# Weight tiles as contiguous blocks laid out by the host, sixteen k tiles by row halves at a part's begin, later square sums, in a three-part transformer block

## The chip, the cores and the metric

The kernel runs on one core of a Trainium2 chip. The metric is the device time of one execution in microseconds (us); before the change the median of three executions is 2004.15 us. All arithmetic is float32: every operand of a large matmul is split into a high and a low part, and one product is three matmuls (high·high, low·high, high·low).

## The reference, cut to what matters

One layer on 256 tokens of width 2048: a gated feed-forward part (FFN1), a mixer (an RWKV7 recurrence beside a pooling branch), and a second feed-forward part (FFN2), each between two RMS norms and with a residual.

```python
D_MODEL, SEQ, D_FF, RWKV_WIDTH, POOL_WIDTH = 2048, 256, 5632, 1024, 1024

def _rmsnorm(x, g):
    y = x * lax.rsqrt(jnp.mean(x * x, axis=-1, keepdims=True) + NORM_EPS)
    return y * g

def _swiglu(x, w_gate, w_up, w_down):
    return (jax.nn.silu(x @ w_gate) * (x @ w_up)) @ w_down

def _hybrid_mixer(u, w_in, ...):
    p = u @ w_in
    z_a, z_b, g_a, g_b = jnp.split(p, IN_SPLITS, axis=-1)
    y_a = _rwkv7_branch(z_a, ...) @ w_proj_a
    y_b = _pool_branch(z_b, pool_w, pool_scale) @ w_proj_b
    m = jax.nn.sigmoid(g_a) * y_a + jax.nn.sigmoid(g_b) * y_b
    return m @ w_out

h = h + 0.5 * _rmsnorm(_swiglu(_rmsnorm(h, ln_ffn1_pre), ffn1_gate, ffn1_up, ffn1_down), ln_ffn1_post)
h = h + _rmsnorm(_hybrid_mixer(_rmsnorm(h, ln_mix_pre), ...), ln_mix_post)
h = h + 0.5 * _rmsnorm(_swiglu(_rmsnorm(h, ln_ffn2_pre), ffn2_gate, ffn2_up, ffn2_down), ln_ffn2_post)
```

## The kernel before

**Tiling.** A weight matrix is used in tiles of 128 rows (one k tile) by 512 columns. Two k tiles make a pair of 512 KB. SyncE (SP) loads a pair into one of five `w32` buffers with one DMA, straight from the weight matrix, so that a partition receives two runs of 2 KB. ScalarE (ACT) casts it to the high part `wH`, VectorE (DVE) subtracts to get the low part `wL`, and TensorE (PE) multiplies it with the activations, two halves (h = 0, 1) of 128 tokens, which are the stationary operand. `wH` and `wL` have five buffers each; other tiles lie in 34 general "units" of 4 KB a partition.

**Feed-forward.** The gate and up matrices are worked in eleven column blocks b = 0 to 10 of 512 columns; gate is called `f`, up is called `l`. For some pairs of k tiles a block uses seven products in place of eight (a Strassen-like step over 2 k tiles x 2 column blocks; one such step is called a quad here). A quad saves one product, three matmuls, and costs DVE extra sums and differences of weights: `t13`, a difference into `va[:, 1]`, and `t4`. `GATE1` and `GATE2` give the number of quads of each block; the first half of a quad of block b (`early`) is worked in block b - 1, the other half (`late`) in block b. The down projection and the mixer's output projection use quads too (`quad`).

**A quad's loads.** `raw4` fills two `w32` buffers, `va` and `vb`, with four DMAs of 256 KB, one for each quarter tile; `late` loads two quarter tiles again.

**A part's begin.** The first gemm of the mixer and of FFN2 (`gemm_tok` with `lead`) works the first `LEAD` k tiles by halves of the tokens: all of them for h = 0, then all for h = 1 (`by_half`); pairs from `STAG` k tiles on are held in units and not in the `wH`/`wL` buffers.

**The head.** FFN1's first gemm starts cold (`head`): x comes transposed (`x_t`), one k tile of x with each weight tile, is scaled by the norm's gain and split. After k tile `SQ` = 11 the square sums of x for the norm are released: four squares on ACT, additions on DVE (`xq`), two small matmuls (`px`), and a power on GpSimd (POOL) that gives `rs`, with which gate's result leaves PSUM.

**What sets the order.** All operations are recorded, and `Plan.simulate` replays them with a cost model (rates of DMA and engines, deadlines, buffers) and so fixes, before the program is built, the order on each engine. On the chip each engine then works its list strictly in order, and waits on semaphores. In the profile nearly all operations therefore carry the one line L494 (the replay in `emit`); they are told apart by the names of their tiles.

Of the kernel before, what the change touches and what calls it, by code (L numbers as in the profile page):

```python
# [38 lines left out]
STAG = 8  # L39
LEAD = 12  # L40
# [9 lines left out]
GATE1 = [0, 0, 2, 4, 3, 4, 3, 4, 3, 4, 4]  # L50
GATE2 = [0, 0, 3, 4, 3, 4, 3, 4, 3, 4, 4]
# [4 lines left out]
SPARE = 1  # L56
HOLD = 3e5
# [9 lines left out]
ONES = 8  # L67
FIRST = 0.4

# [21 lines left out]
SYNC = 55.0  # L91
LAND = 1600.0
LANES = 8
CARRY = 1800.0
# [9 lines left out]
class Plan:  # L104
# [109 lines left out]
    def cost(s, o, name, w, r, k):  # L214
# [4 lines left out]
        if name == "dma_start":  # L219
            x = w[0]  # L220
            o.nbytes = math.prod(x.shape) * 4
            run = min(min(y.shape[-1] for y in w + r) * 4, 2048)
            o.dur = o.nbytes / (387.0 if run >= 2048 else 387.0 * max(run, 64) * 1.25
                                / (run + 512))
            o.pace = {"SP": 500.0, "ACT": 110.0, "POOL": 600.0}[o.eng]
            return
# [66 lines left out]
    def simulate(s):  # L293
# [23 lines left out]
        def can(o):  # L317
            for i in o.new:
# [189 lines left out]
class Block:  # L508
# [183 lines left out]
    def head(s, w, c0, KT, do, keep, xs):  # L692
# [20 lines left out]
        while k < KT:  # L713
            if k:
                first(load, k, n(k))
# [5 lines left out]
        for k in range(KT):  # L721
# [6 lines left out]
            if k == SQ:  # L728
                s.late = last
                with s.set(behind=last, lag=4000.0):  # L730
# [92 lines left out]
class Columns:  # L823
# [32 lines left out]
    def early(s, k):  # L856
        q = s.b
        V = q.nc.vector
        va, vb = q.raw4(k, s.wf, s.cf, s.wl, s.cl)
        t13 = q.unit((P, 2, 512), F32, "t13")  # L860
        V.tensor_tensor(out=t13, in0=va, in1=vb[:, :1].to_broadcast([P, 2, 512]),
# [3 lines left out]
        V.tensor_tensor(out=t4, in0=vb[:, 1], in1=va[:, 1], op=ALU.subtract)  # L865
# [9 lines left out]
    def late(s, k):  # L875
        q = s.b
        vc = q.raw().rearrange("p (a c) -> p a c", a=2)
        for i, (w, c0) in enumerate(((s.wf, s.cf), (s.wl, s.cl))):
# [1119 lines left out]
```

## Time and profile before

| | |
|---|---|
| Median of three executions | 2004.15 us (2002.16 to 2005.69) |
| The profiled execution: its own time, its span | 2001.42 us, 1999.6 us |
| PE busy | 1988.3 us (99%) |
| DVE busy | 1782.8 us (89%) |
| ACT busy | 1179.8 us (59%) |
| POOL busy | 75.4 us (4%) |
| Mean DMA rate | 239 GB/s |
| Granted TensorE clock | 0.999 |

A window row gives, for a stretch of the span, the busy time of each engine with its number of instructions, the granted clock, the share of time in which the 16 DMA engines were busy, and the rate. A matmul's shown duration (0.39 us) overlaps the next one, so a lost time on PE is read from the distance between starts; the timeline shows starts and durations, and in brackets the idle time ahead of an instruction with what ended it. A group row ends in busy time, mean ns of one, idle time before. A DMA row gives instructions, KB and median us from issue to landing.

### The profile page before, as it was taken

Reading aid. Unit: us, or ns where it says so; the run is one execution under the profiler, and the core shown is the slowest. Engines: PE = TensorE matmul, PEld = TensorE weight load, DVE = VectorE, ACT = ScalarE, POOL = GpSimd, SP = SyncE. Lnnn points to the kernel's source line nnn. Section 1 sums busy time; section 2 is a strip of 40 time slices with the busy share of each in tenths; the row PEclk is TensorE's granted clock in tenths of the full one; section 3 lists DMA queues with packets and bytes.
Section 4 is the critical chain, followed back from the end, with each engine's and each line's share of the span. In section 5 each row is a group of like instructions: output and inputs, shape, how many; then the busy total and the mean of one; then the engine's idle time right before and its main releaser. Section 6 shows DMA issues by size and latency. Waiting matters only on the chain.

```text
span 1999.6 us, 28096 instructions
## 1 busy us (share of the span) xinstructions
PE 1988.3 (99%) x9751; PEld 1641.3 (82%) x9751; DVE 1782.8 (89%) x2320; ACT 1179.8 (59%) x1557; POOL 75.4 (4%) x142
## 2 busy tenths in 40 slices
PE   9999999999999999999999999999999999999998
PEld 7888888888888888888888788888888888788886
DVE  8989999999989867898859879898999999998896
ACT  7555556566555656864646445575555655655563
POOL 0000000000000020002200100010000000000000
PEclk9999999999999999999999999999999999999999
DMA  8788888887667787767576567777888888976674
GB/s 282 237 261 267 279 264 283 267 283 229 219 197 255 235 261 233 216 194 244 151 218 183 177 202 228 259 233 244 266 278 262 272 282 274 281 225 212 200 253 147
DMA packets 263198, 477.47 MB, mean 239 GB/s; under 512 B 22928, under 2 KB 50832, under 8 KB 263056
## 3 DMA queue, kind: packets, MB, share of 16 engines
q1 hardware_dynamic: 259536, 466.11, 73.9%
q0 software_dynamic: 3232, 9.44, 1.4%
q8 instruction: 76, 1.25, 0.2%
q14 instruction: 66, 0.54, 0.1%
q10 hardware_dynamic: 288, 0.14, 0.0%
HBM read 447.94 MB, written 26.61 MB: 237 GB/s over the span
## 4 chain that ended last, share of the span: by engine, by line
PE 66%; DVE 15%; DMA 9%; issue 7%; ACT 2%; SPq 1%; POOL 0%; DVEq 0%; ACTq 0%; POOLq 0%
PE mm L494 25%; PE l L494 17%; PE f L494 15%; DVE wL L494 7%; DMA w<-in_ffn_gate_dram 6%; PE p L494 5%; DVE t L494 3%; DMA w<-in_ffn_up_dram 2%; ACT wH L494 2%; DVE w L494 1%; SPq L494 1%; DMA x<-cx 1%; DVE sg L494 1%; DVE hL L494 1%; DVE f L494 1%
## 5 line engine op out<-in xcount | busy, mean ns | idle before, releaser
L494 ACT CAST wH<-w 128x1024 fp32r<-128x1024 f32 (+2 forms) x720 | 745.3, 1043 | 627.7 <-PE mm L494 155.6
L494 DVE TENSOR_TENSOR wL<-w,wH 128x1024 fp32r<-128x1024 f32 (+2 forms) x720 | 860.0, 1206 | 135.0 <-ACT wH L494 130.7
L494 PE MATMUL l<-wL,xH 128*128 128x512 f32 x770 | 300.0, 390 | 0.0
L494 PE MATMUL l<-wH,xL 128*128 128x512 f32 x770 | 299.6, 389 | 0.0
L494 PE MATMUL l<-wH,xH 128*128 128x512 f32 x770 | 299.6, 389 | 0.0
L494 PE MATMUL mm<-wL,xH 128*128 128x512 f32 (+1 forms) x656 | 254.6, 388 | 1.1 <-DVE wL L494 1.0
L494 PE MATMUL mm<-wH,xH 128*128 128x512 f32 (+1 forms) x656 | 254.3, 388 | 0.3 <-ACT xH L494 0.3
L494 PE MATMUL mm<-wH,xL 128*128 128x512 f32 (+1 forms) x656 | 253.8, 387 | 0.0
L494 PE MATMUL f<-wL,xH 128*128 128x512 f32 x644 | 251.0, 390 | 0.4 <-DVE wL L494 0.3
L494 PE MATMUL f<-wH,xH 128*128 128x512 f32 x644 | 250.7, 389 | 0.0
L494 PE MATMUL f<-wH,xL 128*128 128x512 f32 x644 | 250.5, 389 | 0.0
L494 DVE TENSOR_TENSOR t<-w,w 128x1024 f32<-128x1024 f32 (+1 forms) x166 | 168.9, 1017 | 18.4 <-DMA w<-in_ffn_gate_dram 14.1
L494 PEld LDWEIGHTS l<-wL,xH 128*128 128x128 f32 x770 | 144.5, 188 | 31.5 <-DVE wL L494 1.5
L494 PEld LDWEIGHTS l<-wH,xL 128*128 128x128 f32 x770 | 144.6, 188 | 29.8
L494 PEld LDWEIGHTS l<-wH,xH 128*128 128x128 f32 x770 | 144.6, 188 | 29.8
L494 PEld LDWEIGHTS mm<-wL,xH 128*128 128x128 f32 x656 | 123.2, 188 | 26.4 <-DVE wL L494 2.4
L494 PEld LDWEIGHTS mm<-wH,xH 128*128 128x128 f32 x656 | 123.2, 188 | 25.1 <-ACT xH L494 0.7
L494 PEld LDWEIGHTS mm<-wH,xL 128*128 128x128 f32 x656 | 123.2, 188 | 24.3 <-DVE xL L494 0.2
L494 PEld LDWEIGHTS f<-wL,xH 128*128 128x128 f32 x644 | 120.9, 188 | 26.6 <-DVE wL L494 1.7
L494 PEld LDWEIGHTS f<-wH,xL 128*128 128x128 f32 x644 | 120.9, 188 | 25.2
L494 PEld LDWEIGHTS f<-wH,xH 128*128 128x128 f32 x644 | 120.9, 188 | 24.9
L494 DVE TENSOR_TENSOR wL<-t,wH 128x1024 fp32r<-128x1024 f32 x103 | 125.2, 1216 | 3.9 <-ACT wH L494 3.6
(310 smaller groups left out, 2778.8 us busy)
## 6 DMA issues: line engine op xcount, KB each, us to landing
w<-in_w_in_dram SPq DMA_DIRECT2D x128, 512.0 KB, 4.5
w<-in_ffn_up_dram SPq DMA_DIRECT2D x113, 512.0 KB, 4.7
w<-in_ffn_gate_dram SPq DMA_DIRECT2D x109, 512.0 KB, 4.8
w<-in_ffn_down_dram SPq DMA_DIRECT2D x104, 512.0 KB, 4.5
w<-in_ffn_gate_dram SPq DMA_DIRECT2D x197, 256.0 KB, 4.2
w<-in_ffn_up_dram SPq DMA_DIRECT2D x189, 256.0 KB, 4.2
w<-in_ffn_down_dram SPq DMA_DIRECT2D x144, 256.0 KB, 3.9
cx<-T SPq DMA_DIRECT2D x32, 512.0 KB, 3.6
```

The lines of the kernel that those rows point to most:

```text
L494: ins = o.fn(*[real(x) for x in o.a], **{n: real(x) for n, x in o.k.items()})
```

## The change

The host lays out every weight anew: a pair of k tiles by 512 columns is one contiguous block of 128 rows of 4 KB, so that each partition gets one run. For a quad there are three blocks, `(l0, f1)`, `(l1, f0)` and `(f1, l1)`; `raw4` needs two DMAs of 512 KB, `late` one. Gate and up lie in one array, and x is laid out as [128, 16 x 256]; `XLOADS` loads its k tiles in groups of 1, 2, 4, 4 and 4. The quads of a block are now also read by the host. `LEAD` goes from 12 to 16, `STAG` from 8 to 6. The last block has three quads and not four in both feed-forward parts, and FFN2's block 2 four and not three. In the head, the part of the square sums from the small matmuls on (`finish`) is recorded after the first gemm's matmuls. The planner's numbers change: DMA rate, the surcharge on carried tiles (`CARRY`), and a rule that keeps the last four free units from operations of the recurrence that run ahead of their turn.

```diff
-STAG = 8
-LEAD = 12
+STAG = 6
+LEAD = 16
-GATE1 = [0, 0, 2, 4, 3, 4, 3, 4, 3, 4, 4]
-GATE2 = [0, 0, 3, 4, 3, 4, 3, 4, 3, 4, 4]
+GATE1 = [0, 0, 2, 4, 3, 4, 3, 4, 3, 4, 3]
+GATE2 = [0, 0, 4, 4, 3, 4, 3, 4, 3, 4, 3]
+SPARE2 = 4
+XLOADS = {1: 1, 2: 2, 4: 4, 8: 4, 12: 4}
+SQLAG = 4000.0
+class Pairs:
+    def __init__(s, ap, KT, where):
+        s.ap, s.KT, s.where = ap, KT, where
+    def tile(s, b, k, i):
+        r = (b * s.KT // 2 + k // 2) * 3 + i
+        return s.ap[r * P:r * P + P]
+    def get(s, j, n, c0, cw):
+        b, side = s.where(c0 // 512)
+        return s.tile(b, j, side)[:, j % 2 * 512:j % 2 * 512 + n * 512]
+    def quad(s, k, c0, i):
+        return s.tile(s.where(c0 // 512)[0], k, i)
...
+RATE = 410.0
-CARRY = 1800.0
+CARRY = 2000.0
...
-                if i.tag == "u" and o.stream != "chain" and len(slots["u"]) <= SPARE:
+                if i.tag == "u" and len(slots["u"]) <= max(SPARE, SPARE2):
                     q = streams.get("chain")
-                    if q and q[0].nom <= o.nom < q[0].nom + HOLD:
+                    few = len(slots["u"]) <= SPARE
+                    if q and o.stream != "chain" and few and q[0].nom <= o.nom < q[0].nom + HOLD:
+                        return False
+                    if q and o.stream == "chain" and len(slots["u"]) <= SPARE2 \
+                            and o.nom > q[0].nom:
                         return False
...
     def get_w(s, w, j, n, c0, cw, own=False):
         w32 = s.raw(own)
-        s.nc.sync.dma_start(out=w32[:, :n * cw].rearrange("p (k c) -> p k c", k=n),
-                            in_=w[j * P:(j + n) * P, c0:c0 + cw]
-                            .rearrange("(k p) c -> p k c", p=P))
+        s.nc.sync.dma_start(out=w32[:, :n * cw], in_=w.get(j, n, c0, cw))
...
-            if k:
-                first(load, k, n(k))
+            if k in XLOADS:
+                first(load, k, XLOADS[k])
             first(get, k, n(k))
...
-    def raw4(s, k, wf, cf, wl, cl):
-        va, vb = [s.raw().rearrange("p (a c) -> p a c", a=2) for _ in range(2)]
-        for dst, kk, w, c0 in ((va[:, 0], k, wl, cl), (vb[:, 0], k, wf, cf),
-                               (va[:, 1], k + 1, wf, cf), (vb[:, 1], k + 1, wl, cl)):
-            s.nc.sync.dma_start(out=dst, in_=w[kk * P:kk * P + P, c0:c0 + 512])
-        return va, vb
+    def raw4(s, k, w, c0):
+        v = [s.raw() for _ in range(2)]
+        for i in range(2):
+            s.nc.sync.dma_start(out=v[i], in_=w.quad(k, c0, i))
+        return [t.rearrange("p (a c) -> p a c", a=2) for t in v]
...
-        V.tensor_tensor(out=t13, in0=va, in1=vb[:, :1].to_broadcast([P, 2, 512]),
+        V.tensor_tensor(out=t13, in0=va, in1=vb[:, 1:].to_broadcast([P, 2, 512]),
                         op=ALU.subtract)
         V.tensor_tensor(out=va[:, 1], in0=va[:, 0], in1=t13[:, 1], op=ALU.add)
         t4 = s.t4[k] = q.tmp("t4")
-        V.tensor_tensor(out=t4, in0=vb[:, 1], in1=va[:, 1], op=ALU.subtract)
+        V.tensor_tensor(out=t4, in0=vb[:, 0], in1=va[:, 1], op=ALU.subtract)
...
-        for i, (w, c0) in enumerate(((s.wf, s.cf), (s.wl, s.cl))):
-            q.nc.sync.dma_start(out=vc[:, i], in_=w[k * P + P:k * P + 2 * P, c0:c0 + 512])
-        b22, b21 = q.halves(vc)
+        q.nc.sync.dma_start(out=vc, in_=s.wf.quad(k, s.cf, 2))
+        b22, b21 = q.halves(vc.rearrange("p (a c) -> p a c", a=2))
...
-            return lambda h, ps: (pss[i].append(ps), h and ev("fl"[i], pss[i]))
+            return lambda h, ps: pss[i].append(ps)
         s.gemm_tok(wg, 0, at, NKD, hold(0), lead=True, xs=xs)
+        if xs:
+            xs[3]()
+        ev("f", pss[0])
         s.gemm_tok(wu, 0, at, NKD, hold(1))
+        ev("l", pss[1])
...
-                in_=x_t[k * P:(k + n) * P].rearrange("(k p) t -> p k t", p=P))
+                out=xT[k // 4].rearrange("p k t -> p (k t)")[:, k % 4 * S:(k % 4 + n) * S],
+                in_=x_t[:, k * S:(k + n) * S])
...
+            sq.append(a)
+
+        def finish():
+            a = sq[0]
             ps = s.psum("px")
```

What this does to the order on the engines is shown at three places. The first is VectorE in the head, where the last gate weights (`wL_70`, `wL_72`), the first up weights (`wL_86`, `wL_89`, `wL_92`), the additions of squares (`xq`) and the first step of the normalised activations (`nx`) meet. Before:

```order
L494 TENSOR_TENSOR wL_72_361<-w32_48_265,wH_71_352 128x1024
L494 TENSOR_TENSOR nx_125_370<-xH_5_168,xL_6_176 128x1024
L494 TENSOR_TENSOR xq_73_363<-xq_73_363,xq_74_372 128x1024
L494 TENSOR_TENSOR nx_129_389<-xH_7_215,xL_8_227 128x1024
L494 TENSOR_TENSOR xq_75_378<-xq_75_378,xq_76_385 128x1024
L494 TENSOR_TENSOR wL_86_406<-w32_84_276,wH_85_393 128x1024
L494 TENSOR_TENSOR xq_73_363<-xq_73_363,xq_75_378 128x1024
L494 TENSOR_TENSOR wL_89_423<-w32_87_290,wH_88_401 128x1024
```

VectorE at the same place now:

```order
L552 TENSOR_TENSOR wL_72_350<-w32_48_237,wH_71_338 128x1024
L552 TENSOR_TENSOR wL_86_357<-w32_84_247,wH_85_348 128x1024
L552 TENSOR_TENSOR nx_125_368<-xH_5_169,xL_6_178 128x1024
L552 TENSOR_TENSOR wL_89_379<-w32_87_257,wH_88_359 128x1024
L552 TENSOR_TENSOR xq_73_366<-xq_73_366,xq_74_376 128x1024
L552 TENSOR_TENSOR nx_129_398<-xH_7_222,xL_8_227 128x1024
L552 TENSOR_TENSOR xq_75_384<-xq_75_384,xq_76_393 128x1024
L552 TENSOR_TENSOR wL_92_419<-w32_90_272,wH_91_401 128x1024
```

The first two pairs of up weights now stand ahead of the additions of squares, and the four large additions stand behind them in front of the third pair.

The second place is SyncE's list of DMAs at the first quad of FFN1 (`w32_161` and `w32_162` are its two buffers `va` and `vb`; `cx0` and `x32_109` carry the block's result through memory). Before:

```order
L494 DMA w32_158_605<-in_ffn1_gate_dram 128x2x512
L494 DMA w32_161_626<-in_ffn1_up_dram 128x512
L494 DMA w32_161_626<-in_ffn1_gate_dram 128x512
L494 DMA cx0_87<-T1_108_635 128x1024
L494 DMA w32_162_655<-in_ffn1_gate_dram 128x512
L494 DMA w32_162_655<-in_ffn1_up_dram 128x512
L494 DMA x32_109_690<-cx0_87 32x4x256 x4
```

SyncE at the same quad now:

```order
L552 DMA w32_158_591<-in_gate_up1_dram 128x1024
L552 DMA cx0_87<-T1_108_620 128x1024
L552 DMA w32_161_641<-in_gate_up1_dram 128x1024
L552 DMA w32_162_649<-in_gate_up1_dram 128x1024
L552 DMA x32_109_673<-cx0_87 32x4x256 x4
L552 DMA w32_175_728<-in_gate_up1_dram 128x1024
```

Four issues of quarter tiles have become two of whole buffers, and the store of the carried tile has moved ahead of both.

The third place is GpSimd in the mixer, where the first recurrence's four powers (`g`) and the loads of the second recurrence's small weights (`w` from `rwkv_w`, `rwkv_a`, `rwkv_g`) share a queue. Before:

```order
L494 DMA w_2005_8741<-in_rwkv_w_dram 64x512 x2
L494 DMA w_2005_8741<-in_rwkv_a_dram 64x512 x2
L494 DMA w_2096_8768<-in_rwkv_g_dram 128x512
L494 DMA w_2096_8768<-in_rwkv_g_dram 32x512 x3
L494 DMA msp<-sgb_8255 128x512
L494 DMA w_2096_8768<-in_rwkv_g_dram 32x512
L494 COPY Z_7526<-ev_7516 64x256
L494 COPY Z_7526<-od_7520 64x256
```

GpSimd where the same loads stand now:

```order
L552 TENSOR_TENSOR g_1821_8951<-g_1820_8938,mhalf 128x4
L552 TENSOR_TENSOR g_1831_9043<-g_1830_9026,mhalf 128x4
L552 DMA w_1998_9061<-in_rwkv_w_dram 64x512 x2
L552 DMA w_1998_9061<-in_rwkv_a_dram 64x512 x2
L552 DMA w_2089_9091<-in_rwkv_g_dram 128x512
L552 DMA w_2089_9091<-in_rwkv_g_dram 32x512 x4
L552 MEMSET ev_9128 64x8x32
L552 MEMSET od_9136 64x8x32
L552 MEMSET Z_9147 128x512
L552 TENSOR_TENSOR g_1839_9158<-g_1838_9149,mhalf 128x4
```

The nine loads stood ahead of the recurrence's copies and powers and now stand behind its third power, in front of its fourth.

More of the change, by code (lines that the diff above doesn't have):

```diff
@@ L729, in head @@
                 s.late = last
-                with s.set(behind=last, lag=4000.0):
+                with s.set(behind=last, lag=SQLAG):
                     square()
@@ L1050, in down @@
     def down(s, wd, at, KT, ev, hT, sm, plan):
-        for c, (nq, first, step) in ((0, plan[0]), (2, plan[1])):
-            J = Columns(s, wd, c * 512, wd, c * 512 + 512, at, KT, sm,
-                        [2 * i for i in range(nq)], s.bank, s.psum)
+        for c, (nq, first, step), ks in zip((0, 2), plan, down_quads(plan)):
+            J = Columns(s, wd, c * 512, wd, c * 512 + 512, at, KT, sm, ks, s.bank, s.psum)
             quads = list(J.quads)
@@ L1876, in load @@
             if k is None:
[L1877 removed]
+                nc.scalar.dma_start(out=xT[0][:, 0], in_=x_t[:, :S])
                 nc.scalar.dma_start(out=ct[:, :16], in_=cols[:, :16])
@@ L1966, in laid_out @@
         o += n * P
-    return (("x_t", _np.ascontiguousarray(_np.asarray(inputs["x"])[0].T)),
-            ("cols", _np.ascontiguousarray(cols.reshape(NCOL, P).T)))
+    return (("x_t", _np.ascontiguousarray(rows(_np.asarray(inputs["x"])[0].T, 0, S))),
+            ("cols", _np.ascontiguousarray(cols.reshape(NCOL, P).T)),
+            *((n, _np.ascontiguousarray(v, _np.float32)) for n, v in big))
 def kernel(**inputs):
```

116 lines of the change are left out of this document (86 added, 30 removed).

## Prediction

> **What bounds the kernel now.** I read the page's shares first, then the windows by stage, then PE's waits, then the timeline at the places where PE lost time, and last what fed those places. The page:
>
> ```profile
> span 1999.6 us, 28096 instructions
> PE 1988.3 (99%) x9751; PEld 1641.3 (82%) x9751; DVE 1782.8 (89%) x2320; ACT 1179.8 (59%) x1557; POOL 75.4 (4%) x142
> PE 66%; DVE 15%; DMA 9%; issue 7%; ACT 2%; SPq 1%; POOL 0%; DVEq 0%; ACTq 0%; POOLq 0%
> ```
>
> PE is the bound over the whole span and DVE is close behind. The windows say how close PE is to its own pace:
>
> ```profile
> core 0: us, PE busy (x) PEld busy (x) DVE busy (x) ACT busy (x) POOL busy (x), PEclk, DMA share, GB/s
> 10.00:20.00 10.00, 9.43 (x42) 7.50 (x41) 8.23 (x15) 8.24 (x16) 0.00 (x0) 1.00 1.01 355
> 20.00:70.00 50.00, 49.45 (x220) 40.18 (x219) 49.55 (x60) 32.12 (x37) 3.17 (x5) 1.00 0.72 231
> 200.00:300.00 100.00, 100.00 (x442) 82.61 (x442) 93.38 (x105) 58.83 (x72) 0.00 (x0) 1.00 0.84 271
> 400.00:500.00 100.00, 99.84 (x439) 81.92 (x438) 95.95 (x112) 61.38 (x72) 0.00 (x0) 1.00 0.82 256
> 1697.00:1712.00 15.00, 15.00 (x67) 12.40 (x67) 13.04 (x16) 8.87 (x11) 0.00 (x0) 1.00 0.94 284
> 1700.00:1800.00 100.00, 99.26 (x435) 81.09 (x434) 95.68 (x111) 62.40 (x74) 0.00 (x0) 1.00 0.82 252
> ```
>
> In the undisturbed 200 to 300 us PE starts 442 matmuls in 100 us, one each 0.226 us, at the full granted clock. A change of layout cannot make a matmul shorter, so what can be won is time in which PE did not start one. Where it waited in the large products:
>
> ```profile
> PE mm L494 <- DVE wL L494: 1.0, 2, 0.6
> PE f L494 <- DVE wL L494: 0.9, 3, 0.6
> ```
>
> These sums are too small, because the shown 0.39 us of a matmul covers part of a wait. The true loss is the distance of two starts less 0.226:
>
> ```profile
> 17.01 0.39 PE L494 MATMUL mm<-wH,xH 128*128 128x512 f32 x1
> 17.97 0.50 PE L494 MATMUL mm<-wL,xH 128*128 128x512 f32 x1 [0.57 <-DVE wL L494]
> 28.75 0.39 PE L494 MATMUL mm<-wH,xH 128*128 128x512 f32 x1
> 29.59 0.50 PE L494 MATMUL mm<-wL,xH 128*128 128x512 f32 x1 [0.44 <-DVE wL L494]
> 65.67 0.39 PE L494 MATMUL f<-wH,xH 128*128 128x512 f32 x1
> 66.17 0.50 PE L494 MATMUL f<-wL,xH 128*128 128x512 f32 x1
> 420.63 0.40 PE L494 MATMUL f<-wH,xH 128*128 128x512 f32 x1
> 421.18 0.50 PE L494 MATMUL f<-wL,xH 128*128 128x512 f32 x1 [0.15 <-DVE wL L494]
> 1712.05 0.40 PE L494 MATMUL f<-wH,sH 128*128 128x512 f32 x1
> 1713.02 0.50 PE L494 MATMUL f<-wL,sH 128*128 128x512 f32 x1 [0.56 <-DVE wL L494]
> 1716.45 0.40 PE L494 MATMUL f<-wH,xH 128*128 128x512 f32 x1
> 1717.02 0.50 PE L494 MATMUL f<-wL,xH 128*128 128x512 f32 x1 [0.17 <-DVE wL L494]
> ```
>
> The losses are 0.73, 0.61, 0.27, 0.32, 0.74 and 0.34 us, and the matmul behind each wait takes 0.50 in place of 0.39, 0.11 more: 3.0 + 0.7 = 3.7 us in all, always for a low weight part from DVE. That is nearly everything outside the first matmul's wait and the tail, so 0.2% (4 us, about what a measurement of this kernel can tell from no change) is near the most that the profile offers.
>
> **The change part by part.** The sum is made against the profiled execution: 2001.42 us, of which 1999.6 are its span. The median of the runs shown is 2.7 us above it; I come back to that.
>
> *Quads.* FFN1 has one fewer: eight products for seven, three matmuls more, 3 x 0.226 = +0.7 us on PE, on the path. FFN2 moves one from block 10 to block 2: no matmul more or less.
>
> *Blocks 9, where the stalls of 420 and 1712 to 1717 us lie.* DVE had just lost time there to DMA:
>
> ```profile
> 412.95 0.69 DVE L494 TENSOR_TENSOR t<-w,w 128x512 f32<-128x512 f32 x1 [0.87 <-DMA w<-in_ffn_up_dram]
> 1708.80 0.69 DVE L494 TENSOR_TENSOR t<-w,w 128x512 f32<-128x512 f32 x1 [1.42 <-DMA w<-in_ffn_up_dram]
> DVE t L494 <- DMA w<-in_ffn_gate_dram: 14.1, 16, 1.6
> L494 DVE TENSOR_TENSOR t<-w,w 128x1024 f32<-128x1024 f32 x103 | 125.4, 1218 | 14.4 <-DMA w<-in_ffn_gate_dram 14.1
> ```
>
> Each time a `t4` waited for its last quarter tile 4 to 8 us before PE waited for DVE, while the DMA engines were 94% busy (1697 to 1712 us). The change works on both: block 9 now prepares three quads of block 10 and not four, which takes an early half (one difference of 1.22 us, two of 0.69, two low parts of 1.22, by these rows and that of 28.31 us below: 5.0 us of DVE work) and its 1 MB out of the block, and the last quarter comes with its block. Bounds: nothing of these 1.40 + 0.33 = 1.7 us goes, or all; the waits (0.87, 1.42) are smaller than the DVE work that leaves, so I take 1.6.
>
> *One block per load.* At full load the rate can be read:
>
> ```profile
> 22.00:27.00 5.00, 5.00 (x24) 4.14 (x23) 5.00 (x6) 5.00 (x6) 0.00 (x0) 1.00 1.03 394
> 1252.00:1254.00 2.00, 2.00 (x11) 1.65 (x10) 1.69 (x2) 0.84 (x3) 0.00 (x0) 1.00 1.02 416
> w<-in_ffn_gate_dram SPq DMA_DIRECT2D x109, 512.0 KB, 4.8
> w<-in_ffn_down_dram SPq DMA_DIRECT2D x104, 512.0 KB, 4.5
> w<-in_ffn_gate_dram SPq DMA_DIRECT2D x197, 256.0 KB, 4.2
> ```
>
> At 22 to 27 us all loads are pairs in runs of 2 KB (394 GB/s); at 1252 to 1254 us runs of 4 KB lie among them (416). So the new layout is worth 5% of DMA time or somewhat more, and PE does not wait for DMA itself. In undisturbed blocks it gives 0: what hides it is PE's full pace. As a wait saver it counts only in block 9 (above) and the head (below).
>
> The trace also says what a power of two in the row distance costs. The down matrix has rows 8 KB apart and lands in 4.5 us, the gate matrix has rows of 22 KB and takes 4.8: no cost. The Trainium skill, "DMA: Bandwidth & Descriptors", section "Latency and other measured facts", says that rows at large powers of two slow a copy, to 207 GB/s at 512 KB, and advises contiguous tiles. That speaks for the weights and against x, whose rows are now 16 KB apart; the page has no figure for 16 KB. By its 207 GB/s, as an estimate, the first 128 KB of x would land some 0.3 us later than at 355 GB/s, and the sum would be 0.3 us higher. By the rows here it stays as it is.
>
> *The head.* Two of the losses, 0.73 at 17.97 and 0.61 at 29.59 us, with 0.22 for the longer matmuls. What stood ahead of the second on DVE:
>
> ```profile
> 24.91 1.22 DVE L494 TENSOR_TENSOR xq<-xq,xq 128x1024 f32<-128x1024 f32 x1
> 27.18 1.22 DVE L494 TENSOR_TENSOR xq<-xq,xq 128x1024 f32<-128x1024 f32 x1
> 28.31 1.22 DVE L494 TENSOR_TENSOR wL<-w,wH 128x1024 fp32r<-128x1024 f32 x1
> ```
>
> The order puts that `wL` (`wL_86`) ahead of four such operations and the next pair ahead of three, so this stall goes: 0.61 + 0.11. The power that frees gate's result comes later in the list but its inputs are no later than before, and up's matmuls, 96 x 0.226 = 22 us, run meanwhile. The loss at 17.97 us hangs on the first full pair: its weights now come behind 12 k tiles of x and not 10 (4.1 MB and not 3.8), at a rate above the 355 GB/s of 10 to 20 us because x comes in 4 KB runs. 0.3 MB cost 0.8 us, 5 to 15% more rate on 4 MB gains 0.6 to 1.5 us: I take half of the 0.84 as won, 0.4. x4 to x7 in one DMA ahead of the fifth weight tile can delay k = 4 by up to 0.5; I take 0.2. Head: -0.9 (from -1.6 to +0.5; the order of x and weights on SyncE is my count from the change). The square sums' additions now press on the third up pair, which PE wants only 5.4 us after the first; if that cover went, one 1.2 us operation would show.
>
> *The stall at 66 us* (0.27 + 0.11): DVE is full from 20 to 70 us (49.55 of 50), so it moves with DVE's backlog. DVE gets rid of about 1 us of waiting in the head, PE comes 0.9 earlier: -0.2, between -0.4 and +0.5.
>
> *Sixteen k tiles by halves.* PE lost nothing that the waits show at the two part begins, so there is nothing to win. The h = 0 half wants eight pairs in 48 x 0.226 = 10.9 us, eight low parts of 1.22 us need 9.8, and five pairs can now be prepared ahead in units. 0; without that lead up to 2 x 1.2 at each begin.
>
> *GpSimd.* Nine loads of the second recurrence's weights are moved from far ahead of it to just before:
>
> ```profile
> 926.29 1.05 POOL L494 DMA_DIRECT2D w<-in_rwkv_w_dram  x2
> 966.06 1.01 POOL L494 TENSOR_TENSOR g<-g,mhalf 128x4 f32<-128x4 f32 x1
> 971.06 0.28 PE L494 MATMUL pg<-lgs,kH 128*128 128x256 f32 x1
> w<-in_rwkv_a_dram POOLq DMA_DIRECT2D x4, 128.0 KB, 6.7
> ```
>
> They now follow the third power, which before ended at 967.1; the fourth load is issued 3 x 0.53 = 1.6 us later, lands 6.7 after that, and a cast of about 1 us on ACT comes on top: 976.4. PE wants it, by the order, 20 matmuls (4.5 us) behind the last `pg`, which it started at 971.06: at 975.6. Queued behind: on ACT the next weight cast, on POOL the fourth power. +0.5 (0 to +2.5; the old place had 40 us of slack, so no gain).
>
> *Sum.* +0.7 - 1.6 - 0.9 - 0.2 + 0.5 = -1.5 us: 1999.9 for a profiled execution. The three timed runs lie 0.7 to 4.3 us above the profiled one. Matmuls at a fixed clock do not vary; what can are waits of the kind above, where DMA is 94% busy and a late quarter tile reaches PE through DVE. With less DMA time and a lighter block 9 I let 2.2 of the 2.7 us go; this is a choice, its bounds are 0 and 2.7. Median: 2004.15 - 1.5 - 2.2 = 2000.4.
>
> **The rivals.** *The waits only move* (chance 0.25). DVE stays at 95% in the same blocks and the order is new everywhere, so other low parts come late by the same few tenths, and the runs' excess over the profile stays. For it: six places in 2000 us are few, and 66 us is DVE's backlog. Against: the two largest have causes that the change takes away. Then +0.7 + 0.5 and half of the gains remain: 2004.15 + 1.2 - 1.4 = 2004.0.
>
> *DVE becomes the bound through `t13`* (0.20, slower). Before, `t13` needed three quarter tiles and `t4`, two or three operations later, the fourth; now `t13` needs both whole blocks, and behind it on DVE stand low parts that PE wants. Another 256 KB at 284 GB/s are 0.92 us. DVE idles 4.0 to 6.6 us of 100 (95.95 and 93.38 busy); a block of 192 less 3.5 x 3 matmuls takes 41 us, so 100 us hold 8.5 quads, and each may wait 0.5 to 0.8, say 0.62 us, before DVE is full. From there it decides: at 0.72 us for each of the 62 quads of the gate and up blocks PE loses 0.10 x 62 = 6.2 us, 2008.9; at 0.92, 2021. For it: 16 waits of this kind already, up to 1.6 us. Against: they sum to 14.1 us, fewer issues stand between a quad's loads, and the bytes of a quad come 5% faster.
>
> *The change's DMA gain isn't there* is part of the first rival: PE would not see it in undisturbed blocks either way.
>
> **How the numbers follow.** Forecast 0.55, its own range 1997.5 to 2003; waits move 0.25; `t13` 0.20. The border of 0.2% is 2000.1, near the forecast's middle, with its better half wider (all of 3.7 and 2.7 gone, +0.7: 1998.4; some smaller waits on top), so of 0.55 I count 0.42 as faster, and of the first rival 0.05: faster 0.47, same 0.33 (0.13 + 0.20), slower 0.20. The low end, 1997.3, lets the head gain beyond its stalls; the high end, 2007.0, takes in a `t13` wait of 0.69 us.
>
> **What would show it.** Right: no wait for `wL` near 29 us, none above 0.2 us in blocks 9, DMA share near 0.80 where it is 0.84, three matmuls more, timed runs closer together. Wrong in a step: a wait at 18 us as long as now; one of over 1 us at the second recurrence's `pw`; idle time of DVE `t` ahead of DMA that grows from 14.1 us. Wrong as a whole: PE starting fewer than 441 matmuls per 100 us in 200 to 400 us.

## The result and the profile after

The changed kernel takes 2017.6 us (median of five runs, 2013.8 to 2026.3); the kernel before took 2002.2 beside it (2001.1 to 2005.7). The ratio is 1.008, with a 95% interval of 1.0066 to 1.0095: slower by 0.8%. The profiled execution took 2017.61 us, 2015.9 of them its span, 16.3 more than before.

The page of the changed kernel, with its shares and its main DMA queue (packets, MB, share of 16 engines' span):

```profile
span 2015.9 us, 27486 instructions
PE 1995.7 (99%) x9754; PEld 1646.2 (82%) x9754; DVE 1781.2 (88%) x2315; ACT 1178.2 (58%) x1555; POOL 74.3 (4%) x142
q1 hardware_dynamic: 152208, 465.56, 72.6%
```

TensorE is still "99% busy", since a matmul's shown length covers much of a wait behind it. The windows show more (PE busy, matmuls, weight loads, and so on; granted clock, DMA share, GB/s):

```profile
200.00:300.00 100.00, 98.22 (x431) 80.50 (x430) 90.55 (x101) 56.55 (x69) 0.00 (x0) 1.00 0.82 264
300.00:400.00 100.00, 98.61 (x432) 80.51 (x432) 93.62 (x104) 59.62 (x73) 0.00 (x0) 1.00 0.82 272
```

The second of these two rows before the change:

```profile
300.00:400.00 100.00, 100.00 (x443) 82.79 (x442) 96.03 (x109) 61.43 (x75) 0.00 (x0) 1.00 0.86 275
```

431 matmuls in place of 442, and 432 in place of 443: 11 x 0.226 = 2.5 us lost in each 100, in blocks that had lost next to nothing. And the transfers are no faster: 264 GB/s at a share of 0.82 is 322 at full share; before it was 271 at 0.84, 323.

TensorE's waits (engine, tile, what it waited for: us in total, times, longest):

```profile
PE l L552 <- DVE hL L552: 3.8, 3, 1.9
PE l L552 <- DVE wL L552: 3.1, 5, 1.1
PE pa L552 <- ACT sw L552: 2.1, 1, 2.1
PE f L552 <- DVE wL L552: 0.7, 1, 0.7
```

As before these sums are too small. For all kernels below, loss means: the distance from the start of a matmul of 512 columns to the next start, less 0.227 us, summed over a stretch. (Waits between the recurrence's smaller matmuls are not in it.) From before to after it goes 3.1 to 4.0 us in the head (0 to 70 us), 3.1 to 12.3 in the two runs of FFN blocks (200 to 650 and 1450 to 1870), and 9.9 to 15.2 in the mixer between (650 to 1450). That is 0.9 + 9.2 + 5.3 = 15.4 us; the three matmuls more are 0.7. Together 16.1 of the 16.3.

The dearest of the FFN's waits, at 1475.77 us, on three engines in turn (start, length, engine, operation, and in brackets the idle time before it and who ended it):

```profile
1472.79 1.05 ACT L552 CAST wH<-w 128x1024 fp32r<-128x1024 f32 x1 [2.60 <-DMA w<-in_gate_up_dram]
1473.75 1.14 ACT L552 CAST xH<-x 128x512 fp32r<-128x512 f32 x2
1474.79 1.14 ACT L552 CAST hH<-t 128x512 fp32r<-128x512 f32 x2
...
1473.87 1.22 DVE L552 TENSOR_TENSOR wL<-w,wH 128x1024 fp32r<-128x1024 f32 x1 [2.40 <-ACT wH L552]
1475.02 1.28 DVE L552 TENSOR_TENSOR xL<-x,xH 128x512 fp32r<-128x512 f32 x2
1476.22 1.22 DVE L552 TENSOR_TENSOR t<-w,w 128x1024 f32<-128x1024 f32 x1
1477.36 0.68 DVE L552 TENSOR_TENSOR hL<-t,hH 128x512 fp32r<-128x512 f32 x1
...
1475.77 0.39 PE L552 MATMUL l<-hH,xH 128*128 128x512 f32 x1
1478.09 0.50 PE L552 MATMUL l<-hL,xH 128*128 128x512 f32 x1 [1.93 <-DVE hL L552]
1478.43 0.41 PE L552 MATMUL l<-hH,xL 128*128 128x512 f32 x1
1478.67 0.60 PE L552 MATMUL f<-wH,xH 128*128 128x512 f32 x1
1479.07 0.63 PE L552 MATMUL f<-wL,xH 128*128 128x512 f32 x1
```

Read it backwards. TensorE stood for `hL`; VectorE makes its operations in the order of its list, and that `hL` came behind a `wL` that had waited 2.40 us for its cast; ScalarE had stood 2.60 us in front of that cast for a weight block. The block had been issued at 1464.48 and landed at 1472.69, 8.2 us later (half of these loads take under 4.7), because it stood behind the read-back of the carried tile. Behind the wait the clock is halved: eight matmuls 0.43 us apart, 8 x 0.2 = 1.6 us more.

The read-back itself, in the transfers issued in FFN1's block around carried tile 5 (the tiles are counted from 0), before the change and after it (count, size, median us from issue to landing):

```profile
cx<-T SPq DMA_DIRECT2D x1, 512.0 KB, 4.2
x<-cx SPq DMA_DIRECT2D x4, 128.0 KB, 4.3
```

```profile
w<-in_gate_up_dram SPq DMA_DIRECT2D x7, 512.0 KB, 6.8
cx<-T SPq DMA_DIRECT2D x1, 512.0 KB, 4.0
x<-cx SPq DMA_DIRECT2D x4, 128.0 KB, 5.9
```

The store of the tile (`cx<-T`) lands as before, its read-back in four parts 1.6 us later. From the issue of the store to the landing of the last part it was 11.9 us before and is 13.7 now.

### The profile page after: what moved, and what is told of

It reads as the page before. It is cut to its first block, busy times and chain, and to the rows that moved or that the text cites. A ratio compares the mean times of both kernels' runs of the same rounds, so it can differ in the third digit from the quotient of the medians.

```text
span 2015.9 us, 27486 instructions
## 1 busy us (share of the span) xinstructions
PE 1995.7 (99%) x9754; PEld 1646.2 (82%) x9754; DVE 1781.2 (88%) x2315; ACT 1178.2 (58%) x1555; POOL 74.3 (4%) x142
## 4 chain that ended last, share of the span: by engine, by line
PE 76%; DVE 11%; DMA 6%; issue 3%; ACT 3%; SPq 1%; ACTq 0%; DVEq 0%; POOL 0%; POOLq 0%
PE mm L552 24%; PE l L552 23%; PE f L552 22%; PE p L552 5%; DVE wL L552 5%; DMA w<-in_gate_up_dram 4%; ACT wH L552 2%; DVE t L552 1%; DMA w<-in_w_out_dram 1%; SPq L552 1%; DVE xL L552 1%; DVE w L552 1%; DVE AR L552 0%; DMA w<-in_rwkv_g_dram 0%; DVE hL L552 0%
## 5 line engine op out<-in xcount | busy, mean ns | idle before, releaser
L552 ACT CAST wH<-w 128x1024 fp32r<-128x1024 f32 (+1 forms) x711 | 735.3, 1043 | 630.0 <-PE mm L552 160.8
L552 DVE TENSOR_TENSOR wL<-w,wH 128x1024 fp32r<-128x1024 f32 (+1 forms) x711 | 849.4, 1207 | 152.5 <-ACT wH L552 147.6
L552 PE MATMUL mm<-wH,xH 128*128 128x512 f32 (+1 forms) x632 | 246.4, 390 | 0.6 <-ACT xH L552 0.6
L552 PE MATMUL mm<-wH,xL 128*128 128x512 f32 (+1 forms) x632 | 246.9, 391 | 0.0
L552 PE MATMUL mm<-wL,xH 128*128 128x512 f32 (+1 forms) x632 | 245.3, 388 | 0.0
L552 PEld LDWEIGHTS f<-wH,xH 128*128 128x128 f32 x648 | 122.0, 188 | 25.5
```

The source lines that it names most:

```text
L552: ins = o.fn(*[real(x) for x in o.a], **{n: real(x) for n, x in o.k.items()})
```

## The experiments

Ratios are to the kernel before in the same session; the FFN and mixer columns are losses (as above) of the profiled execution.

| kernel | median us | ratio (95%) | head | FFN | mixer |
|---|---|---|---|---|---|
| before | 2002.2 | 1 | 3.1 | 3.1 | 9.9 |
| after | 2017.6 | 1.0080 (1.0066-1.0095) | 4.0 | 12.3 | 15.2 |
| rows2k | 2016.1 | 1.0063 (1.0046-1.0080) | 3.9 | 10.7 | 13.0 |
| carry3500 | 2023.9 | 1.0102 (1.0066-1.0138) | 3.3 | 22.8 | 18.3 |
| warm18 | 2022.3 | 1.0091 (1.0076-1.0107) | 3.2 | 17.3 | 16.4 |
| spare1 | 2013.7 | 1.0052 (1.0035-1.0068) | 2.7 | 15.0 | 12.2 |
| quarters | 2012.0 | 1.0043 (1.0028-1.0058) | 2.6 | 8.7 | 13.1 |
| layout_only | 2015.8 | 1.0071 (1.0051-1.0091) | 3.2 | 14.5 | 11.5 |
| numbers_only | 2005.6 | 1.0015 (1.0005-1.0025) | 3.4 | 3.7 | 11.5 |
| before_sync60 | 2028.5 | 1.0126 (1.0110-1.0141) | 2.8 | 2.0 | 25.5 |
| quarters_387 | 2006.8 | 1.0018 (1.0008-1.0029) | 2.7 | 4.7 | 11.1 |
| quarters_old_numbers | 2005.2 | 1.0009 (1.0000-1.0018) | 2.6 | 4.9 | 10.2 |
| halves | 2005.5 | 1.0013 (1.0004-1.0022) | 2.2 | 5.4 | 11.0 |
| head_only | 2003.4 | 1.0003 (0.9993-1.0012) | 2.5 | 3.1 | 10.9 |
| blocks_387 | 2011.2 | 1.0042 (1.0031-1.0054) | 2.8 | 7.8 | 11.9 |
| last_quarter | 2005.6 | 1.0008 (0.9997-1.0018) | 3.0 | 2.9 | 10.4 |
| split_t13 | 2025.3 | 1.0105 (1.0084-1.0125) | 2.9 | 12.0 | 20.2 |

One profile's losses move by several us where loads are tight: warm18 has after's order but for two transposes, and shows 17.3 for 12.3 in the FFN. So I read pairs with a known difference, and the times with them.

**Row size.** Each block stored as two halves of 128 x 512; order, loads and blocks stay.

```diff
-        return s.ap[r * P:r * P + P]
+        return s.ap[r * P:r * P + 2 * P].rearrange("(a p) c -> p a c", a=2)
```

> The changed kernel in its own order, instruction for instruction, but each block lies in memory as two halves of 128 x 512, so that a load moves rows of 2 KB instead of 4 KB, as before the change. Changed kernel: 2017.6 us. Theory A (the large rows crowd out the small ones): the carried tile's read-back (rows of 1 KB) took 7.8 us from its first issue in FFN1 after the change and 6.7 before, because it now shares the engines with rows of 4 KB; it goes back to about 6.7, the waits of PE for hL in the FFN blocks (some 11 us with the half clock they cause) mostly go, and the time is 2006 to 2010. Theory B (the order that the planner now writes has too little room, whatever the rows are): the waits stay at the same places, the transfers are if anything 5% slower, 2016 to 2023.

The read-backs landed as late as in the changed kernel (7.9 us from first issue in FFN1, 7.8 there), and the FFN lost 10.7 us. Its queue:

```profile
q1 hardware_dynamic: 251792, 465.56, 72.6%
```

Two thirds more packets, the same bytes, the same share: rows of 4 KB are worth nothing here. Theory A fell, and so did the 5% that I had read at two moments of full load.

**When the planner expects the read-back.**

```diff
-CARRY = 2000.0
+CARRY = 3500.0
```

> The changed kernel with one number of the planner altered: a read-back of a carried tile is counted to land 3.5 us later than its transfer, not 2.0, which moves casts and low parts around the carried tile on ScalarE and VectorE and leaves SyncE's loads in the FFN where they are. Theory B (the planner writes the casts of the carried tile, which arrive late, ahead of casts that PE wants first): PE's waits for hL at 253, 294, 378, 1475, 1601 and 1645 us shrink, 2008 to 2013. Theory A (rows): the landings stay as late as they are, something else waits in their place, 2015 to 2020.

Both theories missed: it got worse, 22.8 us in the FFN of the profiled execution (the slowest of the four). My reading, which no run shows by itself: with the carried tile's casts expected later, other casts move ahead of them, and what they delay is wanted sooner. A later due time is no safety by itself.

**Two more warm-up transposes.**

```diff
-WARM = 16
+WARM = 18
```

> The changed kernel with 18 warm-up transposes on TensorE in place of 16: 0.46 us more by the rate of the 16 (3.67 us), which fills most of the 0.58 us that TensorE stood idle before its first product. Theory: the clock was granted in full at 10.9 us and not at 5.1 because of that gap; with it filled the first twelve matmuls take 0.23 us and not 0.43, 2.4 to 2.6 us less in the head, 2015.1. Rival: the gate opens later for another reason, the head stays as it is: 2017.6, and any difference is a matter of runs.

The slow matmuls at the start went from twelve to four, the head's loss from 4.0 to 3.2 us, and the time did not fall. The other kernels with this head and 16 transposes, rows2k apart, had none to four slow ones, and their first product started at 5.3 to 5.5 us, as before the change: in the changed kernel's profile the twelve were chance, about 1 us.

**GpSimd's loads.**

```diff
-SPARE2 = 4
+SPARE2 = 1
```

> The changed kernel with the rule on spare buffers for the recurrence's small weights as it was before the change (SPARE2 1): GpSimd's loads of the second recurrence's weights go out far ahead of it again. Theory: PE's wait of 2.5 us at 987 us for the gate of the second recurrence goes, and with it the 3.4 us at half clock that follow it (1 to 1.7 us): 2013.4 to 2014.5. Rival: the wait is due to casts on ScalarE that queue behind weight casts whatever the time of the loads: then it stays, 2017.6.

The wait for `sw` at 987 us is gone from the profile, the mixer loses 3.0 us less, and the ratio falls from 1.0080 to 1.0052, 5.6 us. The FFN's part stays (15.0).

**The quads' loads by quarter tiles.** The same blocks, loaded in halves of 256 KB:

```diff
-        for i in range(2):
-            s.nc.sync.dma_start(out=v[i], in_=w.quad(k, c0, i))
+        for i, h in ((0, 0), (1, 1), (0, 1), (1, 0)):
+            s.nc.sync.dma_start(out=v[i][:, h * 512:h * 512 + 512],
+                                in_=w.quad(k, c0, i)[:, h * 512:h * 512 + 512])
```

(and the third block in two halves likewise)

> The changed kernel with the blocks of its quads loaded as quarter tiles again: four DMAs of 256 KB for the first two blocks (in the order in which the subtractions want them) and two for the third, all from the new contiguous blocks. Theory C (grain): a load of 512 KB begins to land 3.2 us after its issue and one of 256 KB 2.2 us after it, and a carried tile's read-back stands behind whole blocks where before it stood between halves; in FFN1's block of 276 us it landed 13.7 us after the tile's store, before the change 11.9. With quarters the read-backs land 11 to 12 us after the store, PE's waits in the FFN blocks (12.3 us by distances of matmul starts) fall to 3 to 5, and the time is 2008 to 2010. Rival (numbers of the planner and the new list of quads, not the transfers): nothing changes but the count of DMAs, 2015 to 2020.

5.6 us less in the median (7.4 by the ratios), though TensorE's order differs only in a few rows near 690 us; VectorE's and ScalarE's orders differ more (below). In none of fourteen FFN blocks did the read-back land later than 12.0 us after its store. But the FFN still lost 8.7 us, not 3 to 5: grain was part of it.

**The change's parts, one side at a time.** All planner numbers back, whole blocks kept:

```diff
-STAG = 6
-LEAD = 16
-GATE1 = [0, 0, 2, 4, 3, 4, 3, 4, 3, 4, 3]
-GATE2 = [0, 0, 4, 4, 3, 4, 3, 4, 3, 4, 3]
-SPARE2 = 4
-CARRY = 2000.0
+STAG = 8
+LEAD = 12
+GATE1 = [0, 0, 2, 4, 3, 4, 3, 4, 3, 4, 4]
+GATE2 = [0, 0, 3, 4, 3, 4, 3, 4, 3, 4, 4]
+SPARE2 = 1
+CARRY = 1800.0
-            run = min(min(y.shape[-1] for y in w + r) * 4, 4096)
-            o.dur = o.nbytes / min(RATE, 484.0 * max(run, 64) / (run + 512))
+            run = min(min(y.shape[-1] for y in w + r) * 4, 2048)
+            o.dur = o.nbytes / (387.0 if run >= 2048 else 387.0 * max(run, 64) * 1.25
+                                / (run + 512))
```

> The changed kernel with all of the planner's numbers as before the change: 387 GB/s and runs up to 2 KB, 1.8 us for a read-back, the quads per block, LEAD 12 and STAG 8, the rule on spare buffers. What stays of the change is the layout, the loads by whole blocks, the head. Theory D (numbers): the loss comes from numbers that make the planner expect loads earlier than they come, 2003 to 2007. Theory C (grain of the loads): the FFN's waits stay, 2010 to 2016, less only what the spare-buffer rule gave (some 4 us).

And the other side, the kernel before with the new numbers: the first six lines of this diff the other way round, and the new rule on spare buffers with its `SPARE2`. (The new rate would not reach its rows of 2 KB.)

> The kernel before with the change's numbers alone: 2.0 us for a read-back, the quads per block, LEAD 16 and STAG 6, the rule on spare buffers; its layout, quarter tiles and head stay. Theory D (numbers): most of the loss of 15 us shows here, 2011 to 2016. Theory C (grain): only the recurrence's part shows (the spare-buffer rule, some 4 us), 2004 to 2009.

The numbers alone cost 0.15%; with the old numbers the whole blocks still cost 0.7%. Theory D fell.

**How much an order by itself can cost.** The kernel before, with

```diff
-SYNC = 55.0
+SYNC = 60.0
```

> The kernel before with one number of the planner altered that has nothing to do with the change: 60 ns and not 55 between an engine's end and the next one's start. It writes a slightly different order. Theory E (any other order costs, since waits in this program depend on which low part happens to come late): slower by 3 to 10 us, 2007 to 2014. If the loss belongs to the change itself: within 2 us of the kernel before, 2002 to 2006.

26 us, more than the change and far more than the 3 to 10 of theory E, and none of it in the FFN (2.0). Two rows of TensorE in this kernel:

```profile
1195.48 0.39 PE L494 MATMUL mm<-wH,yL 128*128 128x512 f32 x1
1201.72 0.80 PE L494 MATMUL mm<-wH,yH 128*128 128x512 f32 x1 [5.85 <-ACT yH L494]
```

In the second recurrence TensorE stood 5.85 us for one cast. Earlier in the mixer it had stood 6.14 us for an operation of VectorE (at 1100.43) and 1.84 us for a `wL` (at 1087.17), and stretches at half clock lie beside all three. The mixer's 25.5 holds 15.6 of the 26 us; the rest lies between small matmuls, which the measure leaves out. A planner's list without slack can lose more by a number that nobody thinks about than by the edit under study. So a time alone, without the stage that it was lost in, says little about the edit.

**Grain and rate together.** quarters_387 is quarters with the transfer rate of before, the last five lines of the diff of layout_only; quarters_old_numbers is quarters with that whole diff.

> The changed kernel with the quads' blocks loaded as quarter tiles, as in the run before this one, and with the planner's transfer rate of before (387 GB/s, runs counted up to 2 KB); its other numbers stay the change's. On TensorE and GpSimd the instructions then stand as in the kernel of before with the change's numbers (2005.6 us), but for 8 rows. Theory: the grain of the quads' loads and a rate that the planner took too high are the whole loss in the FFN: PE's waits there fall from 8.7 us to 3 to 4, 2004 to 2007. Rival: rows of 4 KB in the pairs, or the contiguous layout itself, cost what is left: 2010 to 2012.

> The changed kernel with quarter tiles and with all of the planner's numbers as before the change: the order is nearly that of the kernel before, and what is left of the change is the contiguous layout, pairs in rows of 4 KB and the new head. Theory (the layout costs nothing by itself): within 2 us of the kernel before, 2001 to 2004. Rival (layout costs): 2007 to 2010.

Both came back to within 0.2% and 0.1% of the kernel before: the contiguous layout itself gains nothing and costs at most that. The first is also the layout side of numbers_only (2005.6) in the same order on TensorE.

Finer still, with the pairs in two loads too:

```diff
+        m = 1 if isinstance(w, Pairs) else n
+        for i in range(0, n, m):
+            s.nc.sync.dma_start(out=w32[:, i * cw:(i + m) * cw], in_=w.get(j + i, m, c0, cw))
```

> As quarters_387, in the same order, but every pair of the FFN and of the output product is loaded as two DMAs of 256 KB too, from its contiguous block. Theory of the grain, carried on: the read-backs land no later, 10.5 to 11 us after the tile's store (quarters: 11.0), and PE's waits in the FFN fall by another 0.5 to 1.5 us against quarters_387. Rival: some 400 more issues on SyncE at 0.35 to 0.45 us each delay the loads behind them, 3 to 6 us slower than quarters_387.

Nothing more to win (5.4 us lost for 4.7, within what one profile varies), and SyncE's issues hold nothing up: neither the theory nor its rival came.

**The head alone**, put into the kernel before:

```diff
-            if k:
-                first(load, k, n(k))
+            if k in XLOADS:
+                first(load, k, XLOADS[k])
...
-                nc.scalar.dma_start(out=xT[0][:, :1], in_=x_t[:P].unsqueeze(1))
+                nc.scalar.dma_start(out=xT[0][:, 0], in_=x_t[:, :S])
```

(with x's new layout, and `finish` behind gate's product)

> The kernel before with the change's head alone (x laid out by partition, loads of x in groups of 1, 1, 2, 4, 4, 4 k tiles, the square sums finished behind gate's product), in otherwise the same order. The prediction's step: 0.9 us faster, 2001.6. Rival from the traces of the changed kernels, whose losses up to 70 us were 2.5 to 4.0 us where the kernel before had 3.1: nothing won, within 1 us of the kernel before.

1.0003, with an interval from 1.4 us faster to 2.4 us slower: neither expectation is excluded. In the profiled execution the head lost 2.5 us for 3.1.

**Closing the square, and the path.** Whole blocks with the old rate; then the two experiments on `t13`. blocks_387 is the changed kernel with the old rate alone (the five lines again); last_quarter is quarters_387 with the first edit below; split_t13 is the changed kernel with blocks packed as `(l0, f0)` and `(f1, l1)` and the second edit.

```diff
-        for i, h in ((0, 0), (1, 1), (0, 1), (1, 0)):
+        for i, h in ((0, 0), (0, 1), (1, 0), (1, 1)):
...
-        V.tensor_tensor(out=t13, in0=va, in1=vb[:, 1:].to_broadcast([P, 2, 512]), ...)
+        V.tensor_tensor(out=t13[:, 0], in0=va[:, 0], in1=va[:, 1], op=ALU.subtract)
+        V.tensor_tensor(out=t13[:, 1], in0=vb[:, 0], in1=va[:, 1], op=ALU.subtract)
```

> The changed kernel with the planner's transfer rate of before (387 GB/s) and nothing else: with the changed kernel (whole blocks, 410), quarters (quarter tiles, 410) and quarters_387 it makes a square; TensorE's order is that of quarters_387 instruction for instruction. Theory of the grain: whole blocks cost whatever the rate is, PE's waits in the FFN stay at 9 to 15 us (quarters_387: 4.7), 2013 to 2017. Rival (the rate was the cause and quarters only masked it): 2006 to 2009.

> quarters_387 with the quarters of a quad's two blocks in the order l0, f1, l1, f0 in place of l0, f0, f1, l1: the first subtraction now waits for the fourth quarter, as it does with whole blocks, and TensorE, ScalarE, VectorE and GpSimd keep their order exactly. Theory T (the subtraction t13 needs both blocks, and VectorE stands before it): VectorE's waits of t for DMA grow, PE's waits in the FFN rise from 4.7 to 9 to 13 us, 2011 to 2015. Theory R (whole blocks hold up the carried tile's read-back and the loads behind it): no change beyond 1 us, 2005 to 2008.

> The changed kernel with whole blocks that hold l0, f0 and f1, l1, and t13 made by two subtractions of 128 x 512, of which the first needs the first block alone; the second one needs the second block still. VectorE has 0.16 us more work in each quad (0.69 twice for 1.22). Theory T: only the start of the quad is freed, some of the waits go, PE's waits in the FFN fall from 12.3 to 7 to 10 us, 2011 to 2015. Theory R: the read-backs land as late as before, 12 to 14 us after the store in the odd blocks, and the waits stay, 2016 to 2021.

The square, as ratios: whole blocks 1.0080 at 410 GB/s and 1.0042 at 387; quarters 1.0043 and 1.0018. Each of the two edits is worth 0.24 to 0.38%, whatever the other is. blocks_387 lay between its two ranges: the rate counts for more than I gave it, and the grain for something. But the square holds for one set of the other numbers: layout_only has the old rate too, with the old quads, LEAD and spare buffers, and is at 1.0071. Which list the planner writes is worth 0.3% with whole blocks, in ways that I did not take apart.

last_quarter is the cleanest run: four engines keep their order, and `t13` waits for the fourth quarter as with whole blocks. VectorE's waits of `t`, in quarters_387 and then in last_quarter:

```profile
DVE t L553 <- DMA w<-in_gate_up_dram: 10.6, 13, 1.7
```

```profile
DVE t L553 <- DMA w<-in_gate_up_dram: 11.0, 14, 2.2
```

They hardly grow, and the time does not rise. Theory T fell in this form. split_t13 was slower than the change (2025.3), outside both its ranges, and proves less: its order differs, it has more VectorE work, and the mixer lost 20.2 us.

What speaks for theory R, from the records of stores and read-backs of fourteen FFN blocks (tiles 3 to 8 and 27 to 34) in each kernel. In nine kernels with quarter loads, 3 of 126 read-backs landed later than 12.4 us after the store; in six with whole blocks (after, rows2k, warm18, spare1, layout_only, blocks_387) 36 of 84. In those six TensorE then lost, 9 to 24 us behind the store, on average 0.3 us where the read-back took under 12 us (38 blocks), 0.9 for 12 to 13 (20 blocks) and 1.5 above 13 (26). This is a relation over blocks.

Two more kernels with whole blocks limit it. carry3500 had 8 late read-backs of 14. split_t13 had 2, where theory R expected them as late as before, and lost 12.0 us in the FFN all the same: TensorE's waits of `l` for `hL` fell from 3.8 to 0.4 us, those for `wL` rose from 3.1 to 4.7. So a read-back later than 12.4 us is not needed for such a loss.

Nor did the grain vary quite by itself. From after to quarters, and from blocks_387 to quarters_387, the planner also moved some 150 of VectorE's 2315 operations and 36 of ScalarE's 1555, since it writes its lists for the loads that it is given. What three pairs show, each with whole blocks first, is the price of the grain together with its list: 1.0080 and 1.0043, 1.0042 and 1.0018, 1.0071 (layout_only) and 1.0009 (quarters_old_numbers). Whether the read-back, the weight blocks right behind it or that list does the harm inside a block was not separated.

## Why the prediction was wrong

The step that failed is "one block per load", which I counted at 0 in undisturbed blocks: "what hides it is PE's full pace". I asked only what faster transfers would win, not what larger ones would hold up. Before, a quad's tiles came in pieces of 256 KB, and in the block of carried tile 5 the read-back was issued between the two halves of one buffer. Now it stands behind whole blocks of 512 KB, comes up to 2 us later there and late in every other block above all, and in the chain at 1475.77 us a weight block behind it, a cast and TensorE came late in turn. The term is not 0: the FFN lost 9.2 us more in the profiled execution, grain and rate (below) together, and the pairs put 0.24 to 0.6% of the time on the grain with its list. That the read-back is the way is the likeliest reading, not shown (above). The 4 to 7 us in 100 that VectorE had idle, which I had counted for the rival, were no cushion in that chain: a late cast costs where it stands in the list.

The second part of the same step was the rate. I read 394 and 416 GB/s in two moments; over 200 to 300 us the two kernels moved 323 and 322 GB/s per full share. The planner had been told 410, and lists written for it cost 0.25 to 0.38% in the square. The change's numbers stood in the diff, and I looked at none of them for what happens if they are not true. The Trainium skill, "DMA: Bandwidth & Descriptors", section "Rules for kernel authors", asks for 1 MiB or more per DMA for bandwidth. No run here went to 1 MiB, but from 256 to 512 KB there was no bandwidth to gain, and grain was what counted.

The rest, in the order of the prediction:

- *Quads*, +0.7: exact, 9754 matmuls for 9751.
- *Block 9*, -1.6: right in kind. What is left there is 0.37 us at 423.07 (the longer matmul counted, as in the prediction's 1.7) and 0.2 at 1728.9, about 1.2 less than before; it went under in the losses elsewhere.
- *The head*, -0.9: the waits at 17.97 and 29.59 us are gone, as worked out, but two others took the gain in the profiled execution:

```profile
5.71 0.80 PE L552 MATMUL mm<-wH,xH 128*128 128x512 f32 x1 [0.58 <-ACT xH L552]
6.30 0.63 PE L552 MATMUL mm<-wL,xH 128*128 128x512 f32 x1
...
66.22 0.39 PE L552 MATMUL f<-wH,xH 128*128 128x512 f32 x1
67.30 0.50 PE L552 MATMUL f<-wL,xH 128*128 128x512 f32 x1 [0.69 <-DVE wL L552]
```

  The first two rows are mostly the chance told under warm18. The wait at 66 us, where I forecast -0.2, has grown from 0.27 to 0.85, and it is there in every kernel with this head (0.84 or 0.85): VectorE's backlog was, it seems, not worked off but passed on. Eight of the fourteen kernels with this head also lose 0.4 to 0.6 us at a matmul between 7 and 12 us, while x4 to x7 come in one load (before: 0.3 at 8.42); I had given that 0.2. After and rows2k apart, the head loses 2.2 to 3.3 us in these kernels, for 3.1 before: a part of the 0.9, which head_only's interval can neither show nor exclude. Nor can it tell 0.3 us from 0, the estimate that the prediction set beside x's rows of 16 KB.
- *Part begins*, 0: no wait shows there. Two smaller ones in the mixer, 0.34 us at 696.4 and 0.65 at 1276.2, came with the planner's numbers: numbers_only has them too (0.40 and 0.48).
- *GpSimd*, +0.5 (0 to +2.5): the place was right, the size was not.

```profile
970.05 1.10 POOL L552 DMA_DIRECT2D w<-in_rwkv_w_dram  x2
972.17 2.09 POOL L552 DMA_DIRECT2D w<-in_rwkv_g_dram  x4
...
983.38 1.05 ACT L552 CAST kH<-w 128x1024 fp32r<-128x1024 f32 x1 [3.58 <-DMA w<-in_rwkv_g_dram]
989.10 1.18 ACT L552 ACTIVATE sw<-pw,cols 128x256 f32<-128x256 f32 x3
...
989.62 0.39 PE L552 MATMUL pa<-lq,kH 128*128 128x256 f32 x1 [2.13 <-ACT sw L552]
```

  I followed the fourth load to the matmul that needs it. ScalarE waited 3.58 us for a later one, of `g`, with `sw` behind it in its list, and 3.4 us at half clock followed TensorE's wait: 2.3 us by the distance of the starts, and up to 1.7 behind it. spare1 brought 5.6 us by the ratios, more than this place alone; in quarters_387, with the same rule, TensorE does not wait there, so the price hangs on the rest of the list.
- *Runs closer together* (2.2 us let go): the opposite. The runs spread over 12.6 us for 4.6. A list with late loads has more places where a run can lose; that this is the reason is not shown.

Of the rivals, "DVE becomes the bound through t13" had the sign, and its 2008.9 to 2021 held the time, but by another way than its own: the idle time of `t` ahead of DMA, which was to grow from 14.1 us, was 13.0, and last_quarter, with `t13` waiting for the fourth quarter, was no slower than quarters_387. The sign that I had named for "wrong as a whole", under 441 matmuls per 100 us in 200 to 400, came: 431 and 432. Of the signs for right, the three matmuls more and the quiet at 29 us came; the DMA share was 0.82 and not 0.80.

None of these kernels beats the kernel before; the nearest with the new layout is last_quarter, 1.0008.

## What to carry to other kernels

A larger transfer is not free because its engine waits for nothing: ask what small, urgent transfer shares its queue, and which engine keeps its list's order behind that one. A planner's rates are part of a change; hold them against GB/s per DMA share over a long window, not at a peak. And before a loss is explained by an edit, see in which stage it lies, and alter a number that has nothing to do with it: here 5 ns in a planner cost 26 us.

## What the runs showed of the hardware

Half clock followed waits of TensorE of about 2 us (2.13 and 1.93 in the brackets above). Windows of the changed kernel around them (the column behind the engines is the granted clock):

```profile
987.00:990.50 3.50, 1.36 (x8) 0.76 (x7) 3.50 (x9) 3.50 (x9) 0.00 (x0) 1.00 0.54 152
990.70:993.90 3.20, 3.20 (x13) 2.71 (x11) 3.20 (x11) 2.88 (x7) 3.20 (x7) 0.50 0.58 141
...
1478.80:1482.00 3.20, 3.20 (x9) 2.49 (x8) 3.20 (x4) 3.20 (x4) 0.00 (x0) 0.50 0.33 78
1482.20:1486.00 3.80, 3.80 (x19) 3.12 (x18) 3.80 (x4) 3.12 (x6) 0.00 (x0) 1.00 0.90 274
```

The Trainium skill, "TensorE: Matmul & The Clock Gate", section "Why this matters for your kernels", warns of idle gaps above about 3 us; here shorter ones did it. The length alone does not decide: in spare1 half clock (0.50 from 296.3 to 299.5) followed two waits of 0.98 and 1.24 us that ended at 294.0 and 295.8; in warm18 one wait of 2.76 us up to 991.5 was followed by full clock (1.00 from 991.6 to 995), as was one of 2.13 us up to 995.8 in carry3500. In the FFN such a stretch costs about 1.6 us, so one profile's losses hold some chance.

And the four reads of a carried tile (512 KB in rows of 1 KB) with the 512 KB block just ahead of them took 7.1 us in layout_only's block 9 (landed between 408.4 and 415.5 us), while the blocks behind landed 1.2 us apart. In these 7.1 us the DMA engines were 99% busy and moved 233 GB/s, where the changed kernel moved 322 per full share over 200 to 300 us. One block does not show whether the small rows alone are the reason.
